# A decoder trunk on one Trainium2 core: the input projections with tokens as rows and 512 weight columns a matmul, turned afterwards, and branch B's attention ahead of its gate

## The chip, the core and the metric

The kernel runs on one core of one Trainium2 chip. The core's engines are named as in the profile: PE (TensorE, matrix products; PEld is its loading of the stationary operand), DVE (VectorE), ACT (ScalarE), POOL (GpSimd) and SP (SyncE, which here only issues transfers). Each runs its own list of instructions in order and waits for the others by semaphores; transfers are carried out by DMA engines. The metric is the time of one execution on the device in microseconds (us), median of several runs.

## The reference

One layer for 256 tokens of width 2048, all in float32:

```
h = rmsnorm(x); proj = h @ w_in            # w_in: 2048 x 14848
qa, ka, va, ga, qb, kb, vb, gb, xc, gc, mg = split(proj)
ya = moba_attention(qa, ka, va)            # 8 heads of 128
yb = swa_attention(qb, kb, vb, sinks)      # 16 query heads of 64, 4 key heads
yc = rglru_branch(xc, ...)                 # short convolution and a scan over tokens
y  = stack(ya*silu(ga), yb*silu(gb), yc*silu(gc))
x  = x + (sum over branches of sigmoid(mg)*(y @ w_br)) @ w_out
x  = x + sigmoid(rmsnorm(x) @ w_pg) * (p @ w_pp); out = rmsnorm(x)
```

Each branch is 1024 wide, except kb and vb (256 columns each); mg has 2048 columns a branch.

## The kernel before

**Weights.** All weights come in tiles of 128 rows x 1024 columns of float32 (512 KB), loaded through SP's queue (line 103) into four raw buffers. Each tile is split on the chip: ACT rounds it to a reduced-precision part wh (line 118), DVE subtracts to get the rest wl (line 119). The activations are split the same way, and a product is the sum of hi x hi, hi x lo and lo x hi, three matmuls.

**Two forms of projection.** `project` (with `mm3`, lines 150 to 152) holds a 128x128 piece of the activations still and lets 512 weight columns move past it; the result has tokens on the rows. Per weight tile of 512-column chunks that is 12 matmuls of 512 columns. `project_turned` (lines 212 and 214) holds the weights still and lets the activations of all 256 tokens move: hi and lo side by side (512 columns) past wh, hi alone (256 columns) past wl; the result has features on the rows, in chunks of 256 columns. The turned form makes xc, gc, qa, ka, ga, qb, kb and gb (29 chunks of 256), the other makes the values, the merge gates and all later products; vb is one chunk of 256 in the token form. A turned chunk is evacuated by `scaled`: ACT copies one half (line 437), DVE adds the other (line 438) and multiplies by the norm's scale, spread along a row (line 440 or 442). The gates ga and gb then get a sigmoid on ACT and a multiply on DVE.

**Turning.** `flip` turns a token-major block: DVE transposes 32x32 blocks (line 569), SP writes the block to memory (line 571) and reads it back in four strided pieces (line 574); readers take the rest of the permutation through a strided view (`flipped`). Before the change it serves the attention probabilities (flip_b and its like), the merged rows (flip_m) and the updated stream (flip_x).

**Order.** Attention is cut into steps. `hand_out` puts the steps of each pair of heads into `todo`, a pair beginning every so many steps, and `tick`, called after each split of a weight tile, runs one step between the matmuls of that tile. For branch B a pair starts every 6 ticks, and its probabilities get LATE = 3 ticks between turn and use: the scores (s_b), the softmax, the flip, then the cast w_b on ACT (line 598), its low part on DVE (line 599), and the second product py_b on PE. The splits carry a higher priority in the scheduler that sets the order on each engine. Branch B comes after the merge of C and one part of the merge gates: qb, kb, vb, gb are projected, then the merge of A (weights bra, gates sg_a) runs with B's attention between its matmuls, then the merge of B (brb), the output product and the last gate.

## Time and profile before

| | us |
|---|---|
| median of three runs | 1014.35 (1013.31 to 1014.84) |
| the profiled execution | 1014.71 |
| its span in the trace | 1012.9 |
| PE busy | 995.3 |
| DVE busy | 673.1 |
| ACT busy | 549.1 |

Busy times are of the profiled execution. A busy PE is one with a matmul in flight; successive matmuls overlap, so the pitch from start to start, not the length of a record, is what one costs. A stretch in which PE's busy time is below the stretch has PE waiting; what it waited for is in the view of waits.

### The profile page before, as it was taken

How to read it: one execution, taken by the hardware profiler on the slowest of the kernel's cores; microseconds unless marked ns; L12 is line 12 of the kernel's file. 1: busy time of each engine (PE TensorE's matmuls, PEld its weight loads, DVE VectorE, ACT ScalarE, POOL GpSimd, SP SyncE). 2: the span in 40 equal slices, each digit the busy share in tenths (PEclk: the TensorE clock that was granted, in tenths of full speed). 3: DMA queues.
4: the chain of work that ended last, by engine and by line, in shares of the span. 5: the costliest groups of instructions: out<-in, count | busy, mean ns of one | idle time of the engine just before them, and what ended most of it. 6: DMA issues, size and time to landing. Idle time of an engine off the chain costs nothing.

```text
span 1012.9 us, 13571 instructions
## 1 busy us (share of the span) xinstructions
PE 995.3 (98%) x5024; PEld 845.1 (83%) x5024; DVE 673.1 (66%) x993; ACT 549.1 (54%) x767; POOL 15.1 (1%) x14
## 2 busy tenths in 40 slices
PE   9999999999999999999999998999999999999996
PEld 7888888888888888888988877788788888888886
DVE  6766956667867576555456787697656555565764
ACT  8644455557555556544446756766544444454552
POOL 0000000000000000000000001010000000000000
PEclk9999999999999999999999999999999999999999
DMA  9856656554666766666656657867677786779662
GB/s 338 305 190 220 197 187 180 174 177 157 209 208 205 224 209 195 210 198 191 186 190 199 207 188 207 249 190 240 212 238 231 233 283 207 248 259 326 206 192 83
DMA packets 71977, 216.43 MB, mean 214 GB/s; under 512 B 8120, under 2 KB 21352, under 8 KB 71400
## 3 DMA queue, kind: packets, MB, share of 16 engines
q1 hardware_dynamic: 65376, 202.93, 62.3%
q10 hardware_dynamic: 6536, 12.65, 3.6%
q8 instruction: 39, 0.64, 0.3%
q14 instruction: 26, 0.21, 0.1%
HBM read 202.93 MB, written 12.62 MB: 213 GB/s over the span
## 4 chain that ended last, share of the span: by engine, by line
PE 83%; DMA 5%; DVE 5%; issue 2%; ACT 2%; SPq 1%; POOLq 0%; POOL 0%; ACTq 0%; DVEq 0%
PE ps_in L212 21%; PE ps_in L214 11%; PE ps_in L150 8%; PE ps_in L152 8%; PE ps_in L151 8%; DMA turn_b<-d_b 3%; PE ps_out L150 3%; PE ps_out L151 3%; PE ps_out L152 3%; PE ps_pg L151 3%; PE ps_pg L150 3%; PE ps_pg L152 3%; DMA d_b<-flip_b 2%; PE ps_brc L152 1%; PE ps_brc L150 1%
## 5 line engine op out<-in xcount | busy, mean ns | idle before, releaser
L119 DVE TENSOR_TENSOR wl_in<-r_in,wh_in 128x1024 fp32r<-128x1024 f32 x232 | 284.5, 1228 | 177.3 <-ACT wh_in L118 176.8
L118 ACT CAST wh_in<-r_in 128x1024 fp32r<-128x1024 f32 x232 | 242.7, 1049 | 245.8 <-PE ps_in L212 140.6
L212 PE MATMUL ps_in<-h,wh_in 128*128 128x512 f32 x928 | 290.2, 393 | 0.0
L214 PEld LDWEIGHTS ps_in<-h,wl_in 128*128 128x128 f32 x928 | 173.6, 188 | 39.5
L151 PE MATMUL ps_in<-wl_in,h 128*128 128x512 f32 (+1 forms) x480 | 184.1, 383 | 0.6 <-DVE wl_in L119 0.6
L152 PE MATMUL ps_in<-wh_in,h 128*128 128x512 f32 (+1 forms) x480 | 184.4, 384 | 0.0
L214 PE MATMUL ps_in<-h,wl_in 128*128 128x256 f32 x928 | 184.4, 280 | 0.0
L150 PE MATMUL ps_in<-wh_in,h 128*128 128x512 f32 (+1 forms) x480 | 184.3, 384 | 0.0
L212 PEld LDWEIGHTS ps_in<-h,wh_in 128*128 128x128 f32 x928 | 142.5, 188 | 0.4
L151 PEld LDWEIGHTS ps_in<-wl_in,h 128*128 128x128 f32 x480 | 90.5, 189 | 18.4 <-DVE wl_in L119 1.5
L152 PEld LDWEIGHTS ps_in<-wh_in,h 128*128 128x128 f32 x480 | 90.4, 188 | 17.6
L150 PEld LDWEIGHTS ps_in<-wh_in,h 128*128 128x128 f32 x480 | 90.6, 189 | 17.0
L119 DVE TENSOR_TENSOR wl_out<-r_out,wh_out 128x1024 fp32r<-128x1024 f32 x32 | 38.8, 1223 | 25.7 <-ACT wh_out L118 25.7
L119 DVE TENSOR_TENSOR wl_pg<-r_pg,wh_pg 128x1024 fp32r<-128x1024 f32 x32 | 38.9, 1222 | 25.2 <-ACT wh_pg L118 25.0
L151 PE MATMUL ps_pg<-wl_pg,x_hi 128*128 128x512 f32 (+1 forms) x160 | 55.3, 347 | 0.0
L152 PE MATMUL ps_pg<-wh_pg,x_lo 128*128 128x512 f32 (+1 forms) x160 | 55.3, 347 | 0.0
L150 PE MATMUL ps_pg<-wh_pg,x_hi 128*128 128x512 f32 (+1 forms) x160 | 55.3, 347 | 0.0
L118 ACT CAST wh_out<-r_out 128x1024 fp32r<-128x1024 f32 x32 | 33.4, 1051 | 35.9 <-PE ps_out L152 29.9
L118 ACT CAST wh_pg<-r_pg 128x1024 fp32r<-128x1024 f32 x32 | 33.4, 1052 | 32.1 <-PE ps_pg L152 24.7
L150 PE MATMUL ps_out<-wh_out,m_hi 128*128 128x512 f32 x128 | 49.9, 390 | 0.0
L152 PE MATMUL ps_out<-wh_out,m_lo 128*128 128x512 f32 x128 | 49.8, 389 | 0.0
L151 PE MATMUL ps_out<-wl_out,m_hi 128*128 128x512 f32 x128 | 49.8, 389 | 0.0
(250 smaller groups left out, 1237.6 us busy)
## 6 DMA issues: line engine op xcount, KB each, us to landing
r_in<-w_in_dram SPq DMA_DIRECT2D x232, 512.0 KB, 4.2
r_out<-w_out_dram SPq DMA_DIRECT2D x32, 512.0 KB, 4.3
r_pg<-w_pg_dram SPq DMA_DIRECT2D x24, 512.0 KB, 5.1
r_brc<-w_br_dram SPq DMA_DIRECT2D x16, 512.0 KB, 3.6
r_bra<-w_br_dram SPq DMA_DIRECT2D x16, 512.0 KB, 4.1
r_brb<-w_br_dram SPq DMA_DIRECT2D x16, 512.0 KB, 4.7
r_pg<-w_pgt_dram SPq DMA_DIRECT2D x8, 512.0 KB, 3.3
d_b<-flip_b SPq DMA_DIRECT2D x8, 384.0 KB, 3.5
```

Of the source, the lines that this page charges most:

```text
L118: casts.append(nc.scalar.copy(hi[:, c], r[:, c]).ins)
L119: los.append(nc.vector.tensor_tensor(lo[:, c], r[:, c], hi[:, c].bitcast(F32), op=ALU.subtract).ins)
L150: nc.tensor.matmul(ps, ah, bh, start=first, stop=False)
L151: nc.tensor.matmul(ps, ah, bl, start=False, stop=False)
L152: nc.tensor.matmul(ps, al, bh, start=False, stop=last)
L212: nc.tensor.matmul(ps[:, j, :], wh[:, cs[j]], h_both[k], start=k == 0, stop=False)
L214: nc.tensor.matmul(ps[:, j, SEQ:], wl[:, cs[j]], h_act[k][0], start=False, stop=k == KD - 1)
```

## The change

Every turned projection becomes a token-major one of 512 weight columns, with `flip` behind it. `to_features` evacuates a chunk by two ACT instructions that scale by token, and hands the block to `flip`. The readers of q, k, gates and branch C's inputs take the `flipped` view; for xc, ACT copies it into place (`place`). Gate multiplies and that copy run SETTLE = 8 ticks later, by a new list of timers in `tick`. kb and vb share one chunk of 512. The norm's scale is no longer spread along a row. A probability turn gets LATE = 5 ticks, a B pair starts every 7. In branch B the attention pairs are handed out after kb, vb and qb, three empty ticks ahead of them, and gb is projected behind that.

```diff
-LATE = 3
+STEPS = 14
+LATE = 5
 TURN_LATE = 5
-WOFF = 32
+SETTLE = 8
...
+    def later(ticks, work):
+        timers.append([ticks, work])
+
     def tick():
-        if todo:
+        due = []
+        for t in timers:
+            t[0] -= 1
+            if t[0] == 0:
+                due.append(t)
+        timers[:] = [t for t in timers if t[0] > 0]
+        if due or todo:
             with tc.issue_after(casts[-1]), tc.issue_after(los[-1]):
-                todo.pop(0)()
+                for t in due:
+                    t[1]()
+                if todo:
+                    todo.pop(0)()
...
-    def project_turned(row, name):
-        ps = matrix_psum(name)
-        get = weights_of(w_in, row, name, WT // SEQ, WOFF)
-        for k in range(KD):
-            (wh, wl), kk = get(k)
-            cs = [slice(kk * SEQ + j * P, kk * SEQ + (j + 1) * P) for j in range(NH)]
-            for j in range(NH):
-                nc.tensor.matmul(ps[:, j, :], wh[:, cs[j]], h_both[k], start=k == 0, stop=False)
-            for j in range(NH):
-                nc.tensor.matmul(ps[:, j, SEQ:], wl[:, cs[j]], h_act[k][0], start=False, stop=k == KD - 1)
-        return ps
...
+    def as_blocks(t):
+
+        n = t.shape[1] // P
+        return t.rearrange("p (h a q) -> p h a q", h=n, a=4) if n > 1 else t.rearrange("p (a q) -> p a q", a=4)
...
-        dg = small.tile([P, SEQ], F32, tag="dg", name=f"dg_{name}", bufs=1)
-        pb = aux(f"row_{name}")
-        for h in range(NH):
-            nc.vector.tensor_scalar_mul(dg[:, h * P : (h + 1) * P], ident, rs[:, h : h + 1])
-        nc.tensor.matmul(pb[:, :SEQ], ones, dg, start=True, stop=True)
-        row = const.tile([P, SEQ], F32, name=f"row_{name}")
-        nc.scalar.copy(row, pb[:, :SEQ])
-        return rs, row
+        return rs
...
-    rs1, row1 = first["rms"]
+    rs1 = first["rms"]
+    rs_q = {d: const.tile([P, NH], F32, name=f"rs_q{d}") for d in (DA, DB)}
+    for d, t in rs_q.items():
+        nc.vector.tensor_scalar_mul(t, rs1, d ** -0.5)
...
-    def scaled(dst, ps, factor=None):
-        nc.scalar.copy(dst, ps[:, :, :SEQ])
-        nc.vector.tensor_tensor(dst, ps[:, :, SEQ:], dst, op=ALU.add)
-        if factor is None:
-            nc.vector.tensor_tensor(dst, dst, rows(row1, NH), op=ALU.mult)
-        else:
-            nc.vector.scalar_tensor_tensor(dst, dst, factor, rows(row1, NH), op0=ALU.mult, op1=ALU.mult)
-
-    def turned(dst, n, factor=None):
-        for c in range(n):
-            scaled(dst[:, 2 * c : 2 * c + 2, :], in_turned(), factor)
-
-    def silu(dst, n, name):
-        for c in range(0, n, 2):
-            d = dst[:, 2 * c : 2 * c + 4, :]
-            turned(d, 2)
-            s = temp(f"sig_{name}{c}")
+    def to_features(dst, ps, scale, name):
+
+        n = NH * ps.shape[2] // P
+        s = dst.rearrange("p (j h f) -> p h j f", h=NH, f=P)
+        for h in range(NH):
+            nc.scalar.activation(s[:, h], ps[:, h].rearrange("p (j f) -> p j f", f=P), AF.Copy, scale=scale[:, h : h + 1])
+        flip(dst, [(slice(0, n), dst)], n, name)
+
+    def chunk(t, c):
+        return t[:, c * NH * CW : (c + 1) * NH * CW]
+
+    def features(t, scale, name):
+        for c in range(2):
+            to_features(chunk(t, c), in_chunk(), scale, f"{name}{c}")
+
+    def feature_tiles(t):
+        return [flipped(chunk(t, k // 4), 8)[:, NH * (k % 4) : NH * (k % 4 + 1)] for k in range(KB)]
+
+    def silu(d, name):
+        to_features(d, in_chunk(), rs1, name)
+
+        def gate():
+            s = temp(f"sig_{name}").rearrange("p k t -> p (k t)")
             nc.scalar.activation(s, d, AF.Sigmoid)
             nc.vector.tensor_tensor(d, d, s, op=ALU.mult)
+
+        later(SETTLE, gate)
...
-        turned(xp[:, :, CONV - 1 :], 4)
+        for c in range(2):
+            t = temp(f"xc{c}").rearrange("p k t -> p (k t)")
+            to_features(t, in_chunk(), rs1, f"xc{c}")
+
+            def place(c=c, t=t):
+                for h in range(NH):
+                    to = xp[:, 4 * c : 4 * c + 4, CONV - 1 + h * P : CONV - 1 + (h + 1) * P]
+                    nc.scalar.copy(to.rearrange("p j (a q) -> p j a q", a=4), flipped(t, 8)[:, h::NH])
+
+            later(SETTLE, place)
...
-            turned(gs[c], 2)
+            to_features(gs[c], in_chunk(), rs1, f"gc{c}")
...
+            qe = small.tile([P, 2, P], F32, tag="qe", name=f"qe_a{ha}")
+            for j in range(2):
+                nc.scalar.copy(as_blocks(qe[:, j]), qa[ha + j][:, 0])
             chained([mm(scs[j][:, :SEQ], qs[j][a], ks[j][b], n == 0, n == 2)
                      for j in (1, 0) for n, (a, b) in enumerate(((1, 0), (0, 1), (0, 0)))]
-                    + [mm(scs[j][:, SEQ : SEQ + P], qa[ha + j][:, 0:P], ka[ha + j][:, 0:P], True, True) for j in range(2)])
+                    + [mm(as_blocks(scs[j][:, SEQ : SEQ + P]), qe[:, j], ka[ha + j][:, 0], True, True) for j in range(2)])
...
-        hand_out([pair(i) for i in range(NB // 2)], 6)
+        hand_out([pair(i) for i in range(NB // 2)], 7)
...
-        turned(ktiles(qT), 4, DA ** -0.5)
+        features(qT, rs_q[DA], "qa")
         between()
-        turned(ktiles(kT), 4)
+        features(kT, rs1, "ka")
         between()
-        silu(ktiles(g), 2, "ga0")
+        silu(chunk(g, 0), "ga0")
         between()
-        silu(ktiles(g)[:, 4:, :], 2, "ga1")
+        silu(chunk(g, 1), "ga1")
         va = [[vh[:, c, h * DA : (h + 1) * DA] for h in range(NA)] for c in range(NH)]
-        qa, ka = ([ktiles(t)[:, h, :] for h in range(NA)] for t in (qT, kT))
-        return attention_heads(qa, ka, va, g)
+        return attention_heads(feature_tiles(qT), feature_tiles(kT), va, g)
 
     def branch_b():
         qT, kv, g = block("qb"), block("kvb"), block("gb")
-        turned(ktiles(qT), 4, DB ** -0.5)
-        kT = ktiles(kv)[:, :2, :]
+        ps = in_chunk()
+        kT = kv[:, : 2 * SEQ]
         vt = ktiles(kv)[:, 2:4, :]
-        turned(kT, 1)
-        token_values(vt, in_chunk(NKV * DB), 0)
-        silu(ktiles(g), 4, "gb")
-
-        qb = [ktiles(qT)[:, i, :] for i in range(NB // 2)]
-        kb = [kT[:, i, :] for i in range(2)]
-        return attention_pairs(qb, kb, vt, g)
+        to_features(kT, ps[:, :, : 2 * P], rs1, "kb")
+        token_values(vt, ps[:, :, 2 * P :], 0)
+        features(qT, rs_q[DB], "qb")
+        kb = [flipped(kT, 4)[:, NH * i : NH * (i + 1)] for i in range(2)]
+        todo.extend([lambda: None] * 3)
+        z = attention_pairs(feature_tiles(qT), kb, vt, g)
+        for c in range(2):
+            silu(chunk(g, c), f"gb{c}")
+        return z
...
-    parts = [(rng(va, BW), CW), (rng(xc, BW), SEQ), (rng(gc, BW), SEQ), (rng(qa, BW), SEQ), (rng(ka, BW), SEQ),
-             (rng(ga, BW), SEQ), (rng(mg + 2 * D, D), CW), (rng(qb, BW), SEQ), (rng(kb, kvw), SEQ), (rng(vb, kvw), SEQ),
-             (rng(gb, BW), SEQ), (rng(mg, D), CW), (rng(mg + D, D), CW)]
+    parts = [rng(va, BW), rng(xc, BW), rng(gc, BW), rng(qa, BW), rng(ka, BW), rng(ga, BW), rng(mg + 2 * D, D),
+             rng(kb, 2 * kvw), rng(qb, BW), rng(gb, BW), rng(mg, D), rng(mg + D, D)]
```

What this does to the order of instructions is shown at three places. First PE, where the first pair of B stands: its scores s_b0 and its second product py_b0. ps_in168 is the first merge-gate chunk of A, ps_bra0 A's first merge product; before, the pair lies in these.

```order
L152 MATMUL ps_in168_4806<-wh_in168_0_4809,h0_116 128x512
L523 MATMUL s_b00_4846<-k_b0_4815,q_b0_4841 128x256 x2
L523 MATMUL s_b01_4847<-k_b0_4815,q_b0_4841 128x256 x2
L523 MATMUL s_b00_4846<-k_b0_4815,q_b0_4841 128x256
L523 MATMUL s_b01_4847<-k_b0_4815,q_b0_4841 128x256
L150 MATMUL ps_in168_4806<-wh_in168_1_4837,h0_116 128x512
...
L150 MATMUL ps_bra0_5020<-wh_bra0_3_5099,za_hi_2674 128x512
L523 MATMUL py_b0_5080<-w_b0_5077,v_b0_4820 128x512 x2
L523 MATMUL py_b0_5080<-w_b0_5077,v_b0_4820 128x2x128 x2
L151 MATMUL ps_bra0_5020<-wl_bra0_3_5100,za_hi_2674 128x512
```

After, with ps_in152 and ps_in160 the two chunks of the gate gb:

```order
L164 MATMUL ps_in152_4040<-wh_in152_3_4097,h1_117 128x512
L536 MATMUL s_b00_4134<-k_b0_4103,q_b0_4129 128x256 x2
L536 MATMUL s_b01_4135<-k_b0_4103,q_b0_4129 128x256 x2
L536 MATMUL s_b00_4134<-k_b0_4103,q_b0_4129 128x256
L536 MATMUL s_b01_4135<-k_b0_4103,q_b0_4129 128x256
L162 MATMUL ps_in152_4040<-wh_in152_4_4125,h2_118 128x512
...
L162 MATMUL ps_in160_4233<-wh_in160_7_4405,h3_119 128x512
L536 MATMUL py_b0_4415<-w_b0_4412,v_b0_4108 128x512 x2
L536 MATMUL py_b0_4415<-w_b0_4412,v_b0_4108 128x2x128 x2
L163 MATMUL ps_in160_4233<-wl_in160_7_4406,h3_119 128x512
```

The scores moved from the first tile of A's gate to the fourth tile of gb's first chunk, and the second product into the last tile of gb's second chunk. The second pair's product follows eight tiles later; from there on a pair comes every seven tiles.

Second, SP's queue: the write (d_b) and read-back (turn_b) of a pair's probabilities among the weight loads (r_in). Before, at the third pair:

```order
L103 DMA r_in184_0_5475<-w_in_dram 128x1024
L571 DMA d_b2_5335<-flip_b2_5333 128x768
L103 DMA r_in184_1_5503<-w_in_dram 128x1024
L103 DMA r_in184_2_5550<-w_in_dram 128x1024
L574 DMA turn_b2_5332<-d_b2_5335 32x4x192 x4
L103 DMA r_in184_3_5577<-w_in_dram 128x1024
```

After, at the first pair, and then at the third:

```order
L584 DMA d_gb0_4227<-flip_gb0_4225 128x1024
L584 DMA d_b0_4285<-flip_b0_4283 128x768
L103 DMA r_in168_0_4444<-w_in_dram 128x1024
L587 DMA gb_3567<-d_gb0_4227 32x4x256 x4
L587 DMA turn_b0_4282<-d_b0_4285 32x4x192 x4
L103 DMA r_in168_1_4469<-w_in_dram 128x1024
...
L103 DMA r_in176_2_4832<-w_in_dram 128x1024
L584 DMA d_b2_4684<-flip_b2_4682 128x768
L103 DMA r_in176_3_4857<-w_in_dram 128x1024
L587 DMA turn_b2_4681<-d_b2_4684 32x4x192 x4
L103 DMA r_in176_4_4900<-w_in_dram 128x1024
```

Before, two weight loads stand between write and read-back at the third, fifth and seventh pair and one at the others; after, one at every pair, but at the first two the read-back of a chunk of gb stands ahead of turn_b.

Third, ACT in the merge of A, around the cast w_b of a pair's probabilities. sg_a0 is the merge gate's sigmoid, st2b and e_b belong to the exponentials of the next pair, and a table load stands where the function changes. Before, at the first pair:

```order
L118 CAST wh_bra0_3_5099<-r_bra0_3_5097 128x1024
L784 ACT_TABLE_LOAD
L784 ACTIVATE sg_a0_4805<-ps_in168_4806,rs_in_513 128x512 x2
L550 ACT_TABLE_LOAD
L550 ACTIVATE st2b_4804<-st2b_4804 128x4
L553 ACTIVATE e_b1_5005,st1b_4803<-e_b1_5005,st0b_4802 128x2x128
L553 ACTIVATE e_b1_5005,st1b_4803<-e_b1_5005,st0b_4802 128x128
...
L598 CAST w_b0_5077<-turn_b0_4983 128x768
L118 CAST wh_in176_0_5128<-r_in176_0_5126 128x1024
```

After, at the second pair and the third:

```order
L455 ACT_TABLE_LOAD
L455 ACTIVATE sig_gb1_4644<-gb_3567 128x1024
L611 CAST w_b1_4618<-turn_b1_4481 128x768
L118 CAST wh_bra0_0_4671<-r_bra0_0_4669 128x1024
...
L118 CAST wh_in176_0_4790<-r_in176_0_4788 128x1024
L118 CAST wh_in176_1_4808<-r_in176_1_4806 128x1024
L611 CAST w_b2_4812<-turn_b2_4681 128x768
L563 ACT_TABLE_LOAD
L563 ACTIVATE st2b_4039<-st2b_4039 128x4
L566 ACTIVATE e_b3_4721,st1b_4038<-e_b3_4721,st0b_4037 128x2x128
L566 ACTIVATE e_b3_4721,st1b_4038<-e_b3_4721,st0b_4037 128x128
```

At the second pair the cast follows the sigmoid of gb, with a table load ahead of it; at the third it moved ahead of the table load and the next pair's exponentials. Between the projections of branch B and the end of A's merge there are nine table loads before and ten after.

## Rows read from the trace of the kernel before

**Rows 1.** The page: an engine's busy us; a costly group (count | busy us, mean ns).
```profile
PE 995.3 (98%) x5024; PEld 845.1 (83%) x5024; DVE 673.1 (66%) x993; ACT 549.1 (54%) x767; POOL 15.1 (1%) x14
...
L212 PE MATMUL ps_in<-h,wh_in 128*128 128x512 f32 x928 | 290.2, 393 | 0.0
```

**Rows 2.** Windows: stretch; us; busy PE, PEld, DVE, ACT, POOL; PEclk; DMA share; GB/s.
```profile
62.32:291.26 228.94, 228.94 (x1329) 201.04 (x1328) 162.35 (x208) 123.47 (x151) 0.00 (x0) 1.00 0.59 191
...
431.51:543.38 111.87, 111.87 (x673) 99.34 (x672) 63.52 (x63) 49.30 (x57) 0.00 (x0) 1.00 0.61 194
543.38:718.93 175.55, 168.57 (x755) 137.42 (x753) 136.06 (x286) 113.62 (x202) 11.69 (x4) 0.99 0.68 213
718.93:827.73 108.80, 108.80 (x482) 90.12 (x480) 62.68 (x55) 50.97 (x52) 0.00 (x0) 1.00 0.75 242
827.73:914.80 87.07, 87.07 (x390) 72.20 (x389) 54.91 (x69) 42.98 (x58) 0.00 (x0) 1.00 0.73 240
```

**Rows 3.** PE's timeline (start, duration in us): turned steps, then the v chunk.
```profile
64.44 0.62 PE L212 MATMUL ps_in<-h,wh_in 128*128 128x512 f32 x2
...
71.40 0.39 PE L212 MATMUL ps_in<-h,wh_in 128*128 128x512 f32 x1
...
487.27 0.28 PE L150 MATMUL ps_in<-wh_in,h 128*128 128x256 f32 x1
...
498.79 0.62 PE L212 MATMUL ps_in<-h,wh_in 128*128 128x512 f32 x2
```

**Rows 4.** Timeline of PE: the row matmul, and both insertions of a B pair.
```profile
61.01 0.59 PE L269 MATMUL row_in<-dg_in,ones 128*128 128x256 f32 x2
61.44 0.81 PE L398 MATMUL prv<-bias_rows,tab 128*128 128x384 f32 x2
...
563.21 0.88 PE L523 MATMUL s_b<-k_b,q_b 128*128 128x256 f32 x6
563.92 0.39 PE L150 MATMUL ps_in<-wh_in,h 128*128 128x512 f32 x1
...
577.12 0.85 PE L523 MATMUL py_b<-w_b,v_b 128*128 128x512 f32 x4
577.80 0.40 PE L151 MATMUL ps_bra<-wl_bra,za_hi 128*128 128x512 f32 x1
```

**Rows 5.** Groups by form, 431.51 to 718.93: count | busy us, mean ns | idle before.
```profile
L151 PE MATMUL ps_in<-wl_in,h 128*128 128x512 f32 x160 | 63.0, 393 | 0.6 <-DVE wl_in L119 0.6
...
L151 PE MATMUL ps_bra<-wl_bra,za_hi 128*128 128x512 f32 x64 | 24.9, 389 | 0.0
...
L569 DVE STREAM_TRANSPOSE flip_b<-e_b 128x768 f32<-128x768 f32 x8 | 7.8, 972 | 0.1
L599 DVE TENSOR_TENSOR w_b<-turn_b,w_b 128x768 fp32r<-128x768 f32 x8 | 7.7, 959 | 24.7 <-ACT w_b L598 24.6
...
L784 ACT ACTIVATE sg_a<-ps_in,rs_in 128x512 f32<-128x512 f32 x8 | 5.1, 686 | 0.0
...
L438 DVE TENSOR_TENSOR qb<-ps_in,qb 128x512 f32<-128x512 f32 x4 | 2.7, 684 | 0.0
```

**Rows 6.** Waits, 543.38 to 718.93: engine, tile, line <- what it waited for: us, times, longest.
```profile
ACT w_b L598 <- DMA turn_b<-d_b: 12.1, 6, 3.4
...
PE py_b L523 <- DVE w_b L599: 6.1, 4, 2.5
...
PE ps_in L151 <- DVE wl_in L119: 0.6, 1, 0.6
...
PE s_b L523 <- DVE q_b L670: 0.2, 1, 0.2
```

**Rows 7.** Timeline of ACT in merge a, first pair.
```profile
567.96 1.28 ACT L784 ACT_TABLE_LOAD   x1
...
573.71 0.82 ACT L598 CAST w_b<-turn_b 128x768 fp32r<-128x768 f32 x1
```

**Rows 8.** Waits of SP's queue, 718 to 915.
```profile
SPq L574 <- DMA d_m<-flip_m: 6.8, 3, 3.2
```

More of the change, by code (lines that the diff above doesn't have):

```diff
@@ L104, in fetch, with split @@
         raws[name] = r, pieces
[L106 removed]
+    def split(name):
         r, pieces = raws.pop(name)
[L108 to L109 removed]
+        hi = wsp.tile([P, WT], F32R, tag="whi", name=f"wh_{name}")
+        lo = wsp.tile([P, WT], F32R, tag="wlo", name=f"wl_{name}")
         n = WT // pieces
@@ L152, in mm3, with weights_of @@
         nc.tensor.matmul(ps, al, bh, start=False, stop=last)
-    def weights_of(src, row, name, sub, off=0):
+    def weights_of(src, row, name, sub):
         held = {}
@@ L467, in branch_c @@
         z = unit("zc")
-        gs = [temp(f"gc{c}") for c in range(2)]
+        gs = [temp(f"gc{c}").rearrange("p k t -> p (k t)") for c in range(2)]
         for c in range(2):
-            turned(gs[c], 2)
+            to_features(gs[c], in_chunk(), rs1, f"gc{c}")
         for k in range(KB):
@@ L634, in pair @@
             yield
-            nc.vector.tensor_tensor(gate[:, cols(ha, 2)], py, gate[:, cols(ha, 2)], op=ALU.mult)
-            split_act(z, ha, 2, gate[:, cols(ha, 2)])
+            g = flipped(chunk(gate, ha // 4), 8)[:, NH * (ha % 4) : NH * (ha % 4 + 2)]
+            nc.vector.tensor_tensor(g, as_tiles(py), g, op=ALU.mult)
+            split_act(z, ha, 2, g)
         hand_out([pair(ha) for ha in range(0, NA, 2)], 11)
@@ L668, in pair @@
             for j in range(2):
-                nc.scalar.copy(qs[half[j], j, :], qb[i][half[j]])
-                nc.vector.tensor_tensor(qs[half[1 - j], j, :], qb[i][half[j]], qs[half[j], j, :].bitcast(F32), op=ALU.subtract)
+                hi, lo = (as_blocks(qs[half[n], j, :]) for n in (j, 1 - j))
+                nc.scalar.copy(hi, qb[i][half[j]])
+                nc.vector.tensor_tensor(lo, qb[i][half[j]], hi.bitcast(F32), op=ALU.subtract)
             scs = [aux(f"s_b{i}{j}") for j in range(2)]
@@ L688, in pair @@
             for j in range(2):
-                nc.scalar.copy(y[half[j]], py[half[1 - j], j * SEQ : (j + 1) * SEQ])
+                nc.scalar.copy(y[half[j]], as_blocks(py[half[1 - j], j * SEQ : (j + 1) * SEQ]))
             for j in range(2):
-                nc.vector.tensor_tensor(y[half[j]], py[half[j], j * SEQ : (j + 1) * SEQ], y[half[j]], op=ALU.add)
-            gi = gate[:, cols(i)]
+                nc.vector.tensor_tensor(y[half[j]], as_blocks(py[half[j], j * SEQ : (j + 1) * SEQ]), y[half[j]], op=ALU.add)
+            gi = flipped(chunk(gate, i // 4), 8)[:, NH * (i % 4) : NH * (i % 4 + 1)]
             nc.vector.tensor_tensor(gi, y, gi, op=ALU.mult)
             split_act(z, i, 1, gi)
-        hand_out([pair(i) for i in range(NB // 2)], 6)
+        hand_out([pair(i) for i in range(NB // 2)], 7)
         return z
@@ L940 @@
         "maskv": maskv,
-        "w_in": np.concatenate([_pack(win[:, c], cw) for c, cw in parts]),
+        "w_in": np.concatenate([_pack(win[:, c]) for c in parts]),
         "sinks": a["sinks"][0],
```

41 lines of the change are left out of this document (17 added, 24 removed).

## Prediction

> **What bounds the kernel now.** The page comes first: TensorE is busy for 995.3 of 1012.9 us [rows 1], so a change is worth what it takes from TensorE's own stream, and a saving on another engine is worth nothing unless TensorE waits for that engine. The windows come next, cut where TensorE goes from one kind of product to another [rows 2]. In four of the five stretches shown its busy time equals the window and the granted clock is 1.00 (2.4 GHz): it never waits, and the time is instructions times pitch. Only the stretch from 543.38, which carries branch B's attention, has idle time (168.57 of 175.55). So there are two questions: what the new order of operands does to the pitch, and what the earlier attention does to that stage.
>
> **Pitch.** A step of a turned projection (two matmuls of 512 columns, two of 256) is read from its first matmul to the next step's: ten steps from 64.44 to 71.40, 0.696 us each [rows 3]. Token-major matmuls are all 512 wide: the stretch from 718.93 (branch B's merge) is 40 weight tiles of 12 matmuls, 480 in 108.80 us, 226.7 ns each [rows 2]. Three of them carry the same 1536 columns in 680.0 ns. The v chunk of branch B, 96 matmuls of 256 columns between 487.27 and 498.79, gives 120.0 ns each [rows 3]. So 256 more columns cost 106.7 ns and each instruction some 13 ns beside its columns. Fewer, wider instructions are what the change brings TensorE.
>
> **The change part by part.**
> Projections: 928 matmuls of line 212 at two a step [rows 1] are 464 steps, 320 in the stretch from 62.32 (xc, gc, qa, ka, ga) and 144 in that from 431.51 (branch B's projections). Each loses 0.0166 us: 5.3 and 2.4, together 7.7 us. The v columns join k's in one 512-wide chunk, so 96 matmuls become 48: 11.52 - 48 x 0.2267 = 0.64 us. The matmul that spreads the norm's scale along a row falls away: from 61.01 to 61.44 [rows 4], 0.43 us. Sum: 8.8 us, all on TensorE, with no wait to absorb it.
>
> Evacuation: before, each 256 columns cost VectorE an add of 0.684 us [rows 5] and a multiply that I put at the same, 2.7 us per 512 columns. After, ScalarE scales twice 128x512 (0.69 each by the nearest row, the gate sg_a, [rows 5]) and VectorE does one block transpose. flip_b does 768 columns in 0.972 us [rows 5], so 1024 take 1.3. VectorE gains 1.4 us a chunk where TensorE did not wait for it: nothing for the end. Later readers take the turned data through a strided view. w_b already reads such a view, 0.959 us for 768 columns, no dearer per column than the plain add's 0.684 for 512 [rows 5]; I put these at nothing.
>
> DMA: 14 full and one half chunk are written to memory and read back, 1 MB each. In the stretch from 62.32 that is 1.05 MB per 21.8 us, 48 GB/s on top of 191, or 239. That from 718.93 ran at 242 without a wait, with three such turns of the merged rows in it [rows 2]. SP's queue is in order: a turn's read-back waits 3.2 us there at the longest for its write [rows 8], with weight loads queued behind. Those loads run ahead by four raw buffers, and there TensorE lost nothing. I take zero for each of the 15 turns. The other end is a B turn of today: the whole loss of its stage (12.1 us, below) over eight, 1.5 us each. I stay at the low end because the new turns are used a chunk or more later, like the merged rows', while B's are used within some tiles.
>
> The attention of B: the stage holds 160 + 64 steps of three matmuls [rows 5], 672 x 0.2267 = 152.3 us, and eight pairs whose two insertions take 0.71 (563.21 to 563.92) and 0.68 (577.12 to 577.80) [rows 4], 11.1 us. Left of 175.55: 12.1 us lost. TensorE's own waits account for 6.1 + 0.6 + 0.2 [rows 6], most of it for the second product of a pair, which waits for VectorE's w_b; the rest is the pipeline emptied and filled again. Behind w_b stand two causes. ScalarE's cast of w_b waits 12.1 us in all for the read-back turn_b [rows 6]. And it stands in ScalarE's order behind a gate with its two table loads and the exponentials of the next pair: one table load starts at 567.96, the cast only at 573.71 [rows 7].
>
> The change aims at both. A turn gets five weight tiles instead of three before its cast (5.4 us more at 2.72 a tile, against a longest TensorE wait of 2.5), a pair starts every seven tiles instead of six, in three of the eight turns one weight load less stands between write and read-back on SP's queue, and in ScalarE's order several casts of w_b now come ahead of the exponentials. VectorE's load falls too. Its 136.06 us [rows 2] less 56 splits of about 1.22 and four gate multiplies of as much leave 7.8 us a pair. With six tiles a pair VectorE is asked for some 15.8 of 17.7 us, with seven for 17.1 of 20.4.
>
> Against it: two pairs now begin in the chunks of the gate gb. There each eight tiles also bring a turn (1.3) and a gate multiply (1.2): 18.6 of 20.4 us, 91%. The sigmoid of the gate needs one table load more in all than before, and each read-back of gb stands on the same SP queue just ahead of turn_b. I expect 1 to 2 us there, at the second products of the first two pairs, and about 2 us over the other six: 4 us left of 12.1, a gain of 8.1. The ends are 0 left (gain 12.1) and 12.1 left (gain 0). I take a value nearer the low end because the added 5.4 us is twice the longest wait.
>
> A page of the Trainium skill bears on the pitch, "TensorE: Matmul & The Clock Gate", section "Wait — 56ns, not 53.3ns?": by it the fixed cost of a matmul at 2.4 GHz is about 2.5 ns beyond its columns. Here the two pitches give 13 ns [rows 2, 3], and the measurement decides. By the page 512 matmuls less would save about 1.3 us instead of some 7; the rival (c) below needs no page.
>
> **Sum.** 1012.9 - 8.8 - 8.1 = 996.0 us of span. The profiled execution's own time stands 1.8 above its span and 0.36 above the median, so 997.8 and then **997.5 us**. With nothing left in B's stage it is 993.4, with all of it left 1005.5.
>
> **Rivals.**
> (a) B's loss stays. VectorE at 91% in the gate chunks, or ScalarE's in-order queue with the additional table load, holds w_b as today, only one chunk earlier. For it: the wait is a chain of two engines and a DMA, and two of its links get more work. Against: five tiles of slack. It gives 1005 to 1006.
> (b) Slower. Each of the 15 new turns costs what a B turn costs today, 1.5 us, because SP holds back weight loads while it waits for the write, or a chunk's evacuation holds the splits: 22.6 - 8.8 gives 1026.7 of span, 1028 us. It decides from 0.6 us a turn if B's loss stays, from 1.1 if B gains as I expect. Against it: three such turns in the stretch from 718.93 and three in that from 827.73, and TensorE busy throughout both.
> (c) The change doesn't do what it says: the narrow matmuls cost by their columns, and 13 ns is peculiar to those places. Then only the row matmul and B's gain are left: 1012.9 - 0.4 - 8.1 is 1004.4 of span, 1005.8 us. Against it: the three pitches come from long runs without a wait.
>
> **How the numbers follow.** Forecast 0.70, (a) 0.18, (b) 0.06, (c) 0.02, and 0.04 for mishaps that eat the gain just up to no change. A measurement here can tell about 0.2%, or 2 us, from no change: faster 0.90, same 0.04, slower 0.06. The range goes from just under the best case of B's stage to just over its unchanged loss, **992.5 to 1006.5**; it leaves out (b), the mishaps, and the worse part of (a).
>
> **What would show it.** In the profile of the changed kernel: the stage from the first xc chunk to merge c's first chunk at about 223.6 us (228.94 now) with TensorE busy all through; branch B's projections at 226.7 ns a matmul; TensorE's wait for w_b well under 6.1 us in all; ScalarE's wait for turn_b under 12.1. Wrong would be: waits of TensorE for wl_in within projection chunks (rival b), w_b waits of 2 us and more at the first two pairs (rival a), or a pitch of 512-wide projection matmuls above 230 ns (rival c).

## The result

The changed kernel takes 1007.4 us (median of four runs, 1006.1 to 1007.7) against 1013.8 before: 0.9933 of it, 95% interval 0.9916 to 0.9951. The forecast was 997.5, with a range from 992.5 to 1006.5. So the kernel became faster, by 6.4 us where 17 were forecast, and its time lies 0.9 us above the range, nearest to rival (a), which had 1005 to 1006.

The profiled execution of the changed kernel has a span of 1005.8 us. From its page, the busy line of PE and the costliest group of matmuls (line, tile, shape, count | busy us, mean ns | idle before it), to be read beside [rows 1]:

```profile
PE 984.7 (98%) x4510; PEld 819.1 (81%) x4510; DVE 658.2 (65%) x950; ACT 555.5 (55%) x780; POOL 16.5 (2%) x14
...
L163 PE MATMUL ps_in<-wl_in,h 128*128 128x512 f32 x928 | 361.8, 390 | 1.9 <-DVE wl_in L119 1.9
```

There are 514 instructions less on PE, and the projections' matmuls are all of one form. The windows of three stretches, cut as in [rows 2] (us; busy PE, PEld, DVE, ACT, POOL; PEclk; DMA share; GB/s). The first is xc to ga, the second B's projections and the merge of A together (287.42 us before, the sum of two rows of [rows 2]), the third the merge of B:

```profile
62.70:287.76 225.06, 224.09 (x1009) 185.83 (x1008) 146.09 (x175) 127.47 (x154) 0.00 (x0) 1.00 0.71 230
...
427.78:711.78 284.00, 275.10 (x1233) 226.43 (x1232) 199.16 (x336) 163.92 (x260) 13.05 (x4) 1.00 0.70 224
711.78:820.58 108.80, 108.80 (x481) 90.09 (x480) 62.75 (x55) 49.70 (x51) 0.00 (x0) 1.00 0.73 241
```

And the waits of the second of these stretches (us in all, times, longest), to be read beside [rows 6]:

```profile
ACT w_b L611 <- DMA turn_b<-d_b: 21.5, 6, 5.8
...
PE py_b L536 <- DVE w_b L612: 4.4, 3, 3.0
...
PE s_b L536 <- DVE q_b L689: 3.6, 3, 1.9
...
PE ps_in L163 <- DVE wl_in L119: 0.9, 2, 0.5
```

Where some 7 us of span went, from the first matmuls of each stretch in the two timelines of PE:

| stretch | before | after | difference | forecast |
|---|---|---|---|---|
| to the first projection matmul | 17.20 | 18.02 | +0.82 | 0 |
| values, to the first xc matmul | 45.12 | 44.68 | -0.44 | -0.43 |
| xc to ga | 228.94 | 225.06 | -3.88 | -5.3 |
| merge of C, attention A | 140.25 | 140.02 | -0.23 | 0 |
| B's projections and merge of A | 287.42 | 284.00 | -3.42 | -11.1 (3.0 for the pitch, 8.1 for the waits) |
| merge of B to the end of the span | 294.0 | 294.0 | 0.0 | 0 |

The miss is in one row. In that stretch the matmuls' own time is 272.2 us after (five chunks of 96 matmuls are 108.8, and 152.3 + 11.1 as before). Of 284.0, 11.8 us are lost, where 12.1 were before and 4 had been forecast. TensorE's waits there moved rather than went: 4.4 us at w_b, 3.6 at q_b, and ScalarE stands for 21.5 us at the read-back of the probabilities instead of 12.1.

The smaller miss is in xc to ga, a wait of VectorE's wl_in that was not there before:

```profile
262.02 0.61 PE L162 MATMUL ps_in<-wh_in,h 128*128 128x512 f32 x2
263.60 0.50 PE L163 MATMUL ps_in<-wl_in,h 128*128 128x512 f32 x1 [0.97 <-DVE wl_in L119]
```

### The profile page after: what moved, and what is told of

The parts are those of the page before. It is cut to its first block, busy times and chain, and to the rows that moved or that the text cites. A ratio compares the mean times of both kernels' runs of the same rounds, so it can differ in the third digit from the quotient of the medians.

```text
span 1005.8 us, 12594 instructions
## 1 busy us (share of the span) xinstructions
PE 984.7 (98%) x4510; PEld 819.1 (81%) x4510; DVE 658.2 (65%) x950; ACT 555.5 (55%) x780; POOL 16.5 (2%) x14
## 4 chain that ended last, share of the span: by engine, by line
PE 80%; DVE 7%; DMA 5%; ACT 4%; issue 3%; SPq 1%; ACTq 0%; POOLq 0%; POOL 0%; DVEq 0%
PE ps_in L163 17%; PE ps_in L164 17%; PE ps_in L162 17%; PE ps_out L162 3%; PE ps_out L164 3%; PE ps_out L163 3%; PE ps_pg L162 3%; PE ps_pg L163 3%; PE ps_pg L164 3%; DVE wl_in L119 2%; PE ps_brc L162 1%; PE ps_brc L164 1%; PE ps_brb L164 1%; PE ps_brb L162 1%; PE ps_brc L163 1%
## 5 line engine op out<-in xcount | busy, mean ns | idle before, releaser
L163 PE MATMUL ps_in<-wl_in,h 128*128 128x512 f32 x928 | 361.8, 390 | 1.9 <-DVE wl_in L119 1.9
L162 PE MATMUL ps_in<-wh_in,h 128*128 128x512 f32 x928 | 361.8, 390 | 0.0
L164 PE MATMUL ps_in<-wh_in,h 128*128 128x512 f32 x928 | 361.3, 389 | 0.0
L163 PEld LDWEIGHTS ps_in<-wl_in,h 128*128 128x128 f32 x928 | 174.2, 188 | 38.7 <-DVE wl_in L119 3.5
L164 PEld LDWEIGHTS ps_in<-wh_in,h 128*128 128x128 f32 x928 | 174.3, 188 | 36.1
L162 PEld LDWEIGHTS ps_in<-wh_in,h 128*128 128x128 f32 x928 | 174.3, 188 | 35.5
L163 PEld LDWEIGHTS ps_pg<-wl_pg,x_hi 128*128 128x128 f32 x160 | 30.2, 189 | 3.8
L164 PEld LDWEIGHTS ps_pg<-wh_pg,x_lo 128*128 128x128 f32 x160 | 30.2, 189 | 3.8
L162 PEld LDWEIGHTS ps_pg<-wh_pg,x_hi 128*128 128x128 f32 x160 | 30.2, 189 | 3.7
L119 DVE TENSOR_TENSOR wl_brb<-r_brb,wh_brb 128x1024 fp32r<-128x1024 f32 x16 | 19.6, 1223 | 17.2 <-ACT wh_brb L118 17.2
```

Source lines behind the costliest of these rows:

```text
L119: los.append(nc.vector.tensor_tensor(lo[:, c], r[:, c], hi[:, c].bitcast(F32), op=ALU.subtract).ins)
L162: nc.tensor.matmul(ps, ah, bh, start=first, stop=False)
L163: nc.tensor.matmul(ps, ah, bl, start=False, stop=False)
L164: nc.tensor.matmul(ps, al, bh, start=False, stop=last)
```

## The experiments

All times are given against runs of the kernel before on the same chip. "Loss" is B's stretch, from its first projection matmul to the first of the merge of B, less the matmuls' own time in it (272.2 us with token-major projections, 275.3 with turned ones).

| run | time, us | ratio to before | B's stretch | loss |
|---|---|---|---|---|
| before | | | 287.4 | 12.1 |
| after | 1007.4 | 0.9933 | 284.0 | 11.8 |
| gate_late | 1007.9 | 0.9927 | 284.6 | 12.3 |
| proj_only | 1012.7 | 0.9972 | 286.6 | 14.4 |
| order_only | 1009.3 | 0.9940 | 282.5 | 7.2 |
| gate_first | 1007.3 | 0.9924 | 284.3 | 12.1 |
| no_trip_gb | 1005.5 | 0.9910 | 282.7 | 10.5 |
| no_trip_b | 997.6 | 0.9832 | 274.0 | 1.7 |
| pool_queue | 1014.0 | 0.9986 | 285.3 | 13.1 |
| late7 | 999.7 | 0.9855 | 276.0 | 3.8 |
| late9 | 999.5 | 0.9855 | 274.7 | 2.5 |
| late7_raw5 | 999.8 | 0.9858 | 276.6 | 4.3 |
| order_late7 | 1003.3 | 0.9894 | 276.0 | 0.7 |
| before_late5 | 1018.7 | 1.0039 | 291.4 | 16.1 |

The ratio's interval is about 0.0015 to either side, 0.002 for after, proj_only and pool_queue. The stretch is from one profiled execution each.

**First theory: the gate.** In the trace after, ScalarE stands 2.1 us for the read-back of gb's second chunk, loads a table and takes the sigmoid, and only then casts w_b of the second pair, for which TensorE waits 3.0 us. If that heads a chain of lateness, moving the gate must free it.

```diff
-    def silu(d, name):
+    def silu(d, name, settle=SETTLE):
...
-        later(SETTLE, gate)
+        later(settle, gate)
...
-            silu(chunk(g, c), f"gb{c}")
+            silu(chunk(g, c), f"gb{c}", SETTLE + 12 * c)   # ticks until the gate's sigmoid
```

> The changed kernel with one number moved: the sigmoid and multiply of gb's second chunk run 20 weight tiles after it, not 8 (the first chunk's stay). Theory G (ScalarE waits for the read-back of gb's second chunk, then loads a table and takes the sigmoid, with the cast w_b of the second pair queued behind; the late work then runs on into the next pairs): TensorE's wait of 3.0 us for the second pair's w_b goes, its waits for w_b and q_b fall from 8.0 us to under 4, and the time from 1007.4 to 1001 to 1004 us. Theory D (VectorE has too much to do in the gate chunks): the wait stays above 2 us, 1006.5 to 1008. Theory L (the probabilities' own read-back lands too late): the second pair's wait goes, but ScalarE's longest wait for turn_b stays near 5.8 us with TensorE's waits behind it, 1004 to 1006.

The time stayed (1007.9, 0.9927), and so did the wait for the second pair's w_b, 3.6 us. Theory G falls. What came is what theory D had named (a wait above 2 us, 1006.5 to 1008); theory L had let this wait go. But with the gate out of the way, ScalarE met the probabilities' own read-back. The rows are SP's queue (start, us to issue, line, transfer), then ScalarE:

```profile
551.90 1.75 SPq L587 DMA_DIRECT2D gb<-d_gb  x4
553.74 3.74 SPq L587 DMA_DIRECT2D turn_b<-d_b  x4
```

```profile
561.27 0.83 ACT L611 CAST w_b<-turn_b 128x768 fp32r<-128x768 f32 x1 [4.05 <-DMA turn_b<-d_b]
```

The gate's read-back goes first, the four pieces of turn_b follow and take 3.7 us to issue, and the cast begins when the last has landed, 4.05 us after ScalarE was ready.

The same theory with the gate projected first, so that only qb's second chunk is turned beside the pairs:

```diff
-        features(qT, rs_q[DB], "qb")
+        for c in range(2):
+            silu(chunk(g, c), f"gb{c}")
+        to_features(chunk(qT, 0), in_chunk(), rs_q[DB], "qb0")
...
-        todo.extend([lambda: None] * 3)
+        todo.extend([lambda: None] * 5)
         z = attention_pairs(feature_tiles(qT), kb, vt, g)
-        for c in range(2):
-            silu(chunk(g, c), f"gb{c}")
+        to_features(chunk(qT, 1), in_chunk(), rs_q[DB], "qb1")
```

> The changed kernel with gb projected ahead of qb, and the attention pairs handed out ahead of qb's second chunk after five empty ticks, so that the gate's read-back, sigmoid and multiply lie before the first pair's casts. Theory G: no wait of TensorE for the first two w_b, 1000 to 1003 us. Theory D: VectorE has a turn but no gate multiply in that chunk, 1003 to 1005. Theory L: ScalarE's waits for turn_b stay at 20 us in all and the time at 1005 to 1007.

1007.3 us and a loss of 12.1: the waits for the first two w_b all but went (0.2 us is left), others came later in the stretch (1.7 us at a later w_b, 2.0 and 1.0 at q_b). This speaks against G as well and is what theory L expected.

**The two parts apart.** The new projections with B's old order, and the old projections with the new one:

```diff
-STEPS = 14
-LATE = 5
+STEPS = 13
+LATE = 3
...
-        hand_out([pair(i) for i in range(NB // 2)], 7)
+        hand_out([pair(i) for i in range(NB // 2)], 6)
...
-        todo.extend([lambda: None] * 3)
-        z = attention_pairs(feature_tiles(qT), kb, vt, g)
         for c in range(2):
             silu(chunk(g, c), f"gb{c}")
-        return z
+        return attention_pairs(feature_tiles(qT), kb, vt, g)
```

> The changed kernel's projections with branch B's order, lateness and period as in the kernel before. If the two parts are independent and the new order brings nothing: the loss of B's stretch stays at 12 us and the time is 1006 to 1008 (the kernel before at 1013.8, less 8.2 for the instructions, plus 1.2 for the stall in the gate ga). If the new order costs what the earlier turns gain: under 1005. If the new order brings what was forecast and the new projections eat it: over 1010.

1012.7 us, 0.9972, some 3 us better than before. That is the time of the third reading (over 1010): behind the old order the new projections bring less than half of the 8.2 us of their instructions. Ahead of attention they bring what they bring after the change (272.45 us from the first projection matmul to the first score of attention A, 276.81 before), but the loss of B's stretch grows from 12.1 to 14.4 us. Its runs scatter more than most (1009.8 to 1015.5). Lateness 3 also holds for branch A here, and TensorE waited 1.7 us for one of A's casts, which it does not after the change.

```diff
-STEPS = 13
-LATE = 3
+STEPS = 14
+LATE = 5
...
-        hand_out([pair(i) for i in range(NB // 2)], 6)
+        hand_out([pair(i) for i in range(NB // 2)], 7)
...
-        return attention_pairs(qb, kb, vt, g)
+        todo.extend([lambda: None] * 3)
+        z = attention_pairs(qb, kb, vt, g)
+        silu(ktiles(g), 4, "gb")
+        return z
```

(gb's four turned chunks come last; q, k and v change places, with the weight columns.)

> The kernel before, with turned projections, but branch B in the new order (k and v, q, three empty ticks, attention, then the gate; lateness 5, period 7, 14 steps). Here gb needs no read-back. Theory G: the loss of B's stretch falls from 12.1 to under 6 us, the time from 1013.8 to 1006 to 1009. Theory D (VectorE still adds and multiplies for the turned gate chunks, 2.7 us each eight tiles, so its load there is no lower): loss 10 or more, 1012 to 1015. Theory L: the longest wait of ScalarE for turn_b stays above 5 us, 1010 to 1012.

The new order alone brings 6 us, more than half of the forecast for it, and 4.9 of them in B's stretch. None of the theories had all of it right: the time is G's, the loss of 7.2 is between G's and D's, and the wait above 5 us that theory L named did not come (3.1 at the longest). Which part of the edit brought the gain, the order, the lateness or the period, was not taken apart; the lateness alone is tested at the end of this section. What is left are the waits at w_b and q_b, and 19 us of ScalarE at turn_b:

```profile
ACT w_b L598 <- DMA turn_b<-d_b: 19.0, 8, 3.1
...
PE s_b L523 <- DVE q_b L670: 2.1, 2, 1.1
...
PE py_b L523 <- DVE w_b L599: 1.5, 3, 0.9
```

**Second theory: the trip.** Theory L says that the probabilities' way through memory takes longer than the lateness covers. It was tested from both sides: with no trip, and with more room.

```diff
         for at, src in srcs:
             nc.vector.transpose(...)
+        if dst is None:       # B's pairs: read the transposed tile itself
+            return t
...
```

> The changed kernel in which the eight pairs of B read their probabilities from the tile that VectorE transposed, without write and read-back (their values are then wrong; VectorE and ScalarE do all they did). Theory L (what is lost is the time that the probabilities' trip takes, with ScalarE standing on it): ScalarE's 21.5 us of waits for turn_b go, and the loss of B's stretch falls from 11.8 to under 3 us, 8 to 10 us faster. Theory D: at most a third of the loss goes, 2 to 4 us faster, and TensorE's waits for q_b stay.

997.6 us, and the loss is 1.7. TensorE's waits of that stretch, all of them, and its window:

```profile
PE s_b L536 <- DVE q_b L694: 0.3, 1, 0.3
PE ps_in L163 <- DVE wl_in L119: 0.2, 1, 0.2
```

```profile
427.52:701.49 273.97, 273.45 (x1233) 226.84 (x1232) 198.93 (x336) 165.05 (x260) 13.06 (x4) 1.00 0.65 209
```

VectorE has the same work in it as after the change (198.9 against 199.2 us busy) in 10 us less, and TensorE waits 0.5 us for it in all. Theory D falls: the load on VectorE and ScalarE is not what costs the time. The waits at q_b go with the trip too, so they were its consequence.

```diff
-STEPS = 14
+STEPS = 16
...
-        for _ in range(LATE):
+        for _ in range(LATE + 2 * name.startswith("b")):
```

> The changed kernel with seven weight tiles in place of five between a pair's turn and its cast in branch B (16 steps a pair). Theory L: ScalarE's waits for turn_b fall from 21.5 to under 8 us, TensorE's for w_b go, the loss of B's stretch falls by 5 to 8 us. Theory D: ScalarE waits less but the waits for q_b and wl_in stay; 0 to 3 us faster.

999.7 us, 0.9855 (0.9839 to 0.9872): faster than both kernels. The trips and their transfers are all still there, so it is their lateness and not their load that had cost the time. ScalarE's wait for turn_b falls from 21.5 to 0.2 us:

```profile
PE py_b L536 <- DVE w_b L612: 0.9, 1, 0.9
...
PE s_b L536 <- DVE q_b L689: 0.3, 1, 0.3
...
ACT w_b L611 <- DMA turn_b<-d_b: 0.2, 1, 0.2
```

```profile
427.40:703.44 276.04, 274.44 (x1234) 226.57 (x1233) 198.20 (x336) 165.27 (x260) 13.06 (x4) 1.00 0.74 230
```

```diff
-        for _ in range(LATE + 2 * name.startswith("b")):    # late7
+        for _ in range(LATE + 4 * name.startswith("b")):    # STEPS 18
```

> As late7, with nine weight tiles of lateness in branch B (18 steps). Theory L with the trip covered at seven: B's stretch stays within 1 us of the 276.0 of late7 and the time within 1.5 us of its 0.9855 of the kernel before. If seven still leaves some pairs short: another 1 to 2 us.

The same time. B's stretch takes 274.7 us, 1.3 less than in late7 and so a little more than the 1 us that was expected; 0.9 of it is lost again ahead of the first projection matmul (18.53 against 17.60 us). Seven tiles are nearly enough.

**How much of the trip the change itself caused.** The gate's two chunks without their trip:

```diff
             nc.vector.transpose(...)
+        if name.startswith("gb"):
+            return            # gb is not written to memory and not read back
```

> The changed kernel without the trip of gb's two chunks through memory (write and read-back left out, the block transposes stay; the gate's values are then wrong). Theory Q (the gate's trip and those of the first two pairs share SP's queue and the transfers, so the probabilities come back late): TensorE's 3.0 us wait for the second pair's w_b goes, the loss of B's stretch falls from 11.8 to about 7 us as with turned projections in the new order, about 4.5 us faster than the changed kernel. Theory D (VectorE and ScalarE, loaded to 85 or 90 per cent and waiting for one another in order, lose the time wherever something is late): the first waits go but others grow, under 2 us faster.

About 2 us faster than the changed kernel (0.9910 against 0.9933, the intervals overlap), 1.3 of it in B's stretch. TensorE's first waits went (at the first two pairs it waits for no w_b), but the third pair's wait grew from 1.05 to 2.2, and ScalarE's sum at turn_b went only from 21.5 to 19.5 us:

```profile
ACT w_b L613 <- DMA turn_b<-d_b: 19.5, 7, 7.2
...
PE s_b L536 <- DVE q_b L691: 2.9, 2, 1.9
...
PE py_b L536 <- DVE w_b L614: 2.5, 2, 2.2
```

So the collision that theory Q names is there, and it is the small part: the time is nearer to what theory D had named (others grow, under 2 us) than to theory Q's 4.5.

```diff
-        flip(dst, [(slice(0, n), dst)], n, name)
+        flip(dst, [(slice(0, n), dst)], n, name, nc.gpsimd)   # write and read-back on POOL's queue
...
```

> The changed kernel with the 15 new turns' write and read-back issued by POOL's queue, so that SP's has the weight loads and the pairs' turns alone. If SP's in-order wait holds the weights back in the stretch of xc to ga: the stall of 1.2 us at wl_in there goes. Theory Q by the queue: the loss of B's stretch falls to about 7 us; both together 5 to 6 us faster. If it is the transfers themselves that share the DMA engines: nothing goes in B's stretch, 0 to 2 us faster. If POOL's way of issuing is slow or holds up VectorE: slower.

Slower than the changed kernel, at the time of the kernel before (0.9986, runs from 1009.1 to 1016.8). The waits of TensorE over the whole span:

```profile
PE py_b L536 <- DVE w_b L612: 4.7, 4, 2.8
...
PE ps_in L163 <- DVE wl_in L119: 1.2, 1, 1.2
```

Neither the stall at wl_in nor the waits at w_b went when the turns left SP's queue; others came (the stretch with attention A took 142.3 us instead of 137.3 from its first score on). In this kernel POOL's queue is the wrong place for these, and SP's in-order wait is not what the stall comes from.

**The new projections without the waits.**

```diff
-STEPS = 14
+STEPS = 16                                   # on order_only
...
-        for _ in range(LATE):
+        for _ in range(LATE + 2 * name.startswith("b")):
```

> The kernel before, turned projections kept, with branch B in the new order and seven weight tiles of lateness: late7 without the new projections. If the projections' part is what was forecast and independent of the rest: 8.2 + 0.4 us of instructions, less the 1.1 us stall, so 6.5 to 8.5 us slower than late7, at 1006 to 1008 (about 0.993 of the kernel before), and B's stretch at 278 to 280 (3 to 5 lost of a floor of 275.3). If the trips of gb still cost something in late7, B's stretch loses 1 us less here than there.

1003.3 us, 3.6 above late7: about half of what was expected. In this kernel TensorE does not wait once in B's stretch; its window is all busy:

```profile
431.59:707.58 275.99, 275.99 (x1425) 236.23 (x1424) 203.17 (x349) 166.61 (x261) 13.05 (x4) 1.00 0.64 214
```

It takes 276.0 us, as late7 does with matmuls that are 3.1 us shorter. From its first projection matmul to the first score of attention A, late7 takes 272.50 us and this kernel 276.82. So the new projections bring 4.3 us ahead of attention, as in the changed kernel, and none in B's stretch, where what their matmuls save is lost to waits that the turned form has not.

**The stall in xc to ga.**

```diff
-    wraw = ctx.enter_context(tc.tile_pool(name="wraw", bufs=4))
+    wraw = ctx.enter_context(tc.tile_pool(name="wraw", bufs=5))   # on late7
```

> As late7, with five raw weight buffers in place of four. If the stall of 1.1 us at wl_in in the chunk of ga comes from weights that arrive late for want of a free buffer: it goes, and the time falls by 1 to 2 us against late7. If it is VectorE's row of scans that stands ahead of the split: the stall stays at about 1 us and the time is that of late7.

The stall stays at 0.98 us, and the time is that of late7 (0.9858). The rows are of ScalarE, VectorE and TensorE (a row's bracket is the idle time before it and its cause):

```profile
259.12 1.05 ACT L118 CAST wh_in<-r_in 128x1024 fp32r<-128x1024 f32 x1 [1.66 <-PE ps_in L164]
```

```profile
257.88 4.18 DVE L521 TENSOR_TENSOR_SCAN xcT<-rg,ig 128x256 f32<-128x256 f32 x7
261.98 1.20 DVE L119 TENSOR_TENSOR wl_in<-r_in,wh_in 128x1024 fp32r<-128x1024 f32 x1
```

```profile
263.23 0.50 PE L163 MATMUL ps_in<-wl_in,h 128*128 128x512 f32 x1 [0.98 <-DVE wl_in L119]
```

The cast is done at 260.17, but the split's low part comes only at 261.98, behind seven scans of branch C that take 4.2 us in a row on VectorE. It is VectorE's order, neither a buffer nor a transfer. Before, eight scans in a row (4.8 us) passed without a stall; why they fell differently there was not tried.

**More room without moving the attention.**

```diff
-STEPS = 13
+STEPS = 15                                   # on the kernel before
...
-        for _ in range(LATE):
+        for _ in range(LATE + 2 * name.startswith("b")):
```

> The kernel before with one number moved: five weight tiles of lateness in branch B in place of three (15 steps), attention still behind the gate, period still six. Theory L: the waits for w_b (6.1 us) fall to under 2, the loss of B's stretch from 12.1 to 6 to 9, 3 to 6 us faster, though the last pair runs over the end of its room by a step. If the period of six tiles is what is too short (VectorE asked for 15.8 of 17.7 us): the loss stays above 10 us.

Slower, 1.0039 (1.0024 to 1.0054), with a loss of 16.1: theory L's numbers were wrong here, and the other reading, that six tiles a pair are too short, fits better. The waits for w_b fell only from 6.1 to 4.1 us, and six waits for the weights' low part came:

```profile
PE ps_in L151 <- DVE wl_in L119: 5.2, 6, 1.1
...
PE py_b L523 <- DVE w_b L599: 4.1, 3, 3.0
```

From the flip to VectorE's part of w_b a pair had 11.5 us on average here, 12.1 before, and over the eight pairs 26 weight splits stood between the two instead of 30: two more steps of lateness gave the trip no time at all. In late7 the added steps come with the period of seven, for which the change made room by starting the attention earlier, and there they pay. That they need that period is likely, but no run had seven tiles of lateness with a period of six.

## Why the prediction was wrong, point by point

**Pitch: right.** A chunk of 96 matmuls goes from its first matmul at 84.47 to the next chunk's at 106.22:

```profile
84.47 0.39 PE L162 MATMUL ps_in<-wh_in,h 128*128 128x512 f32 x1
...
106.22 0.39 PE L162 MATMUL ps_in<-wh_in,h 128*128 128x512 f32 x1
```

That is 226.6 ns each, and B's chunks ahead of its attention take the same 21.76 us. The rule of the Trainium skill in "TensorE: Matmul & The Clock Gate", "Wait — 56ns, not 53.3ns?", with its 2.5 ns beside the columns, does not describe these streams: by the trace it is some 13. The row matmul's 0.44 us came too.

**Flips at nothing: nearly right ahead of attention.** Of 5.3 us in xc to ga, 3.9 came. 1.2 went to the one stall shown above, of a kind that the prediction had looked for under rival (b) as a held-back transfer; it is VectorE's order instead. Rival (b) itself, 1.5 us at each of 15 turns, is refuted: ten turns in this stretch, one stall.

**B's waits: the step that failed.** The sentence was: "A turn gets five weight tiles instead of three before its cast (5.4 us more at 2.72 a tile, against a longest TensorE wait of 2.5)". Two things were wrong in it, and a third beside it.

The first is the 5.4 us. Lateness is counted in steps of the program, one for each weight tile, and in the program's order the two added steps put five splits of weights (line 119) between a pair's flip and its cast where three were. What the trip gets is the distance on the engines. On VectorE the trace has 3, 4, 4, 4, 4, 4, 4, 3 splits between flip and low part of w_b before, and 4, 4, 3, 4, 4, 4, 4, 4 after: 30 and 31, so over all eight pairs a single split was added. The second pair, before and then after:

```profile
587.87 0.97 DVE L569 STREAM_TRANSPOSE flip_b<-e_b 128x768 f32<-128x768 f32 x1
...
589.97 1.21 DVE L119 TENSOR_TENSOR wl_in<-r_in,wh_in 128x1024 fp32r<-128x1024 f32 x1
...
591.85 1.22 DVE L119 TENSOR_TENSOR wl_in<-r_in,wh_in 128x1024 fp32r<-128x1024 f32 x1
...
593.26 1.22 DVE L119 TENSOR_TENSOR wl_in<-r_in,wh_in 128x1024 fp32r<-128x1024 f32 x1
...
596.55 1.23 DVE L119 TENSOR_TENSOR wl_in<-r_in,wh_in 128x1024 fp32r<-128x1024 f32 x1 [1.99 <-ACT wh_in L118]
...
600.01 0.96 DVE L599 TENSOR_TENSOR w_b<-turn_b,w_b 128x768 fp32r<-128x768 f32 x1 [1.95 <-ACT w_b L598]
```

```profile
548.08 0.94 DVE L582 STREAM_TRANSPOSE flip_b<-e_b 128x768 f32<-128x768 f32 x1
548.94 1.18 DVE L119 TENSOR_TENSOR wl_in<-r_in,wh_in 128x1024 fp32r<-128x1024 f32 x1
...
551.57 1.22 DVE L119 TENSOR_TENSOR wl_in<-r_in,wh_in 128x1024 fp32r<-128x1024 f32 x1
...
553.71 1.22 DVE L119 TENSOR_TENSOR wl_in<-r_in,wh_in 128x1024 fp32r<-128x1024 f32 x1
...
556.68 1.22 DVE L119 TENSOR_TENSOR wl_in<-r_in,wh_in 128x1024 fp32r<-128x1024 f32 x1 [1.75 <-ACT wh_in L118]
...
562.28 0.95 DVE L612 TENSOR_TENSOR w_b<-turn_b,w_b 128x768 fp32r<-128x768 f32 x1
```

The time from the start of the flip to the start of the low part did not grow either: 12.1 us on average before (10.1 to 14.5), 11.8 after (8.9 to 14.8). In late7 it is 5.5 splits and 16.0 us, in late9 7.75 and 22.4, and there ScalarE's waits for turn_b are gone (0.2 us in late7, none in late9). This was to be read in VectorE's order of instructions ahead of the run. Why the two steps did not show on the engine was not looked into.

The second is the measure. A longest wait of 2.5 us on TensorE does not say how much is missing, because ScalarE had been hiding part of it. Before, the cast stood behind a gate, two table loads and the next pair's exponentials [rows 7]. The change put it ahead of them, which the prediction counted as a gain. As long as the data has not landed it can turn into a loss: ScalarE stands at the cast, and everything behind it in order stands too. No run moved the cast alone; what such a wait holds up is in the rows. The third pair after the change, on ScalarE, VectorE and TensorE:

```profile
571.28 2.00 ACT L118 CAST wh_in<-r_in 128x1024 fp32r<-128x1024 f32 x2
579.12 0.83 ACT L611 CAST w_b<-turn_b 128x768 fp32r<-128x768 f32 x1 [5.83 <-DMA turn_b<-d_b]
579.97 1.28 ACT L563 ACT_TABLE_LOAD   x1
```

```profile
569.65 0.98 DVE L582 STREAM_TRANSPOSE flip_b<-e_b 128x768 f32<-128x768 f32 x1
...
579.99 0.96 DVE L612 TENSOR_TENSOR w_b<-turn_b,w_b 128x768 fp32r<-128x768 f32 x1 [3.10 <-ACT w_b L611]
```

```profile
581.09 0.93 PE L536 MATMUL py_b<-w_b,v_b 128*128 128x512 f32 x4 [1.05 <-DVE w_b L612]
...
592.85 0.47 PE L536 MATMUL s_b<-k_b,q_b 128*128 128x256 f32 x2 [1.86 <-DVE q_b L689]
```

The flip ends at 570.63, the cast, which waits for the last piece, begins at 579.12, 8.5 us later, and the cast and the low part take another 1.8. ScalarE idles 5.83 us meanwhile, with the exponentials and the next weights' casts queued behind. TensorE waits 1.05 us for this pair, and twelve us later 1.86 (then 1.02) for a q_b that VectorE reached late. One pair, one late landing, some 4 us.

In the changed kernel the five other trips that ScalarE waited for took 7.0 to 10.5 us from the end of the flip to the cast; before, those that it waited for took 8.3 to 12.7. So these trips did become shorter, as the one weight load less had suggested, and it did not help.

The third is the price of the new turns beside the pairs, for which the prediction had put 1 to 2 us at the first two pairs. At the same order, lateness and period B's stretch loses 7.2 us with turned projections (order_only) and 11.8 with the new ones, 4.6 more. Leaving out the trip of gb gives back 1.3 of them (no_trip_gb); where the other 3.3 come from stays open.

**Rival (a): the time nearly right, the mechanism wrong.** It had 1005 to 1006 us, 1.4 below what was measured, with VectorE at 91% in the gate chunks, or the additional table load, holding w_b. no_trip_b has the same VectorE work and no wait for w_b; gate_late takes the gate's sigmoid away from the cast and changes nothing. What is true of it is the gate's trip beside the pairs': 1.3 us (no_trip_gb). Of the signs named ahead, the one for (a) did show, a wait of 3.0 us at the second pair, and ScalarE's wait for turn_b went the wrong way, to 21.5 us; TensorE's sum at w_b alone, 4.4 under 6.1, would have misled.

**The sum, done again.** With enough room the loss of B's stretch falls to 3.8 us (late7), which happens to be the 4 that was forecast for five tiles. The time is then 999.7, 2.2 above the forecast of 997.5. The span of late7 is 997.4, 1.4 above the forecast's 996.0: 1.2 is the stall and 0.4 a later first projection matmul (17.60 against 17.20), with small gains elsewhere. The rest lies between profiled executions and medians: before, the profiled one stood 0.36 above its median, which the forecast took over, and in late7 it stands 0.53 below. The chance of 0.18 for (a) was too small: the argument against it was the five tiles of slack, and that had not been read from an order.

**What stays open.** In B's stretch the token-major form still loses 3.1 us in late7 beyond the turned form's 0.7. With five tiles of lateness no_trip_gb puts some of the difference on the gate's trip; with seven it was not taken apart. The time to the first projection matmul varied from 17.2 to 18.5 us among these traces, with no order in it, and 0.8 us of the difference between the two profiled executions is that.

## What to carry to other kernels

A lateness that the program counts in steps is worth what it puts between the two instructions on the engines: count there, and set the number of microseconds beside the trip's own time from flip to landing plus the work that follows it. An engine that waits for a transfer holds up everything queued behind it (here 5.83 us of ScalarE at one cast, then 1.05, 1.86 and 1.02 us of TensorE), so moving the waiting instruction forward helps only when the data is there. And when a stream of matmuls has no waits, fewer and wider instructions pay by their pitch, as here ahead of attention, but only where nothing else in the stretch takes it back.
